# Seven products for the second feed-forward, and a longer run-up to the state-space scan

## The chip, the cores and the metric

The kernel is one launch on one core of a Trainium2 chip. The metric is the device time of a launch in microseconds (us); lower is better. PE is the matrix engine (TensorE), DVE is VectorE, ACT is ScalarE, POOL is GpSimd; SP issues most transfers.

## What is computed

1024 tokens of width 1024 pass through two attention layers and then a second block; the change lies in the second block. All arithmetic is to fp32 accuracy. Cut to what matters:

```
h = h + 0.5 * swiglu(rms_norm(h, ffn1_norm), ...)        # feed-forward 1
u = rms_norm(h, mix_norm)
q, k, v, s_in, gates = split(u @ w_in)                   # the mixer
y_attn = neighbourhood_attention(q, k, v) @ w_attn_out
y_ssm  = s5_branch(s_in) @ w_ssm_out                     # two scans, GELU, GLU
h = h + (sigmoid(g_attn) * y_attn + sigmoid(g_ssm) * y_ssm) @ w_out
h = h + 0.5 * swiglu(rms_norm(h, ffn2_norm), w_gate, w_up, w_down)   # feed-forward 2
h = h + (p @ w_proj) * sigmoid(rms_norm(h, ple_norm) @ ple_w_gate)   # last stage
out = rms_norm(h, final_norm)

swiglu(x) = (silu(x @ w_gate) * (x @ w_up)) @ w_down     # inner width 2816
```

## The kernel before

**Products.** An fp32 operand is kept as a high and a low part (`whi`, `wlo` for weights, `xh`, `xl` for activations), and `mm3` (L188) makes one product of three matmuls: high by high, high by low, low by high (L194 to L196). Accumulators live in PSUM banks named G, S, T and O. `weights` (L162) loads a raw tile (`wraw`) on SP's queue and splits it: POOL writes the high part (L184), POOL or DVE the low part (L186). A PSUM result is split by `split_ps` (L152): ACT writes the high part (L156), DVE the low part (L157).

**Order.** The code is written once in program order; a scheduler that works with its own time estimates orders each engine's instructions and the slots of each pool. `later(n)` marks instructions as filler that may be put off. Each engine runs its list in order, and each instruction waits for semaphores of what it reads or overwrites.

**Mixer** (`mix`, L1304). `ssm_scan` (L1165) loads its input `ssm_u` in eight pieces (L1172), forms the scan's driving terms by PE (L1183, result copied by ACT, L1189), and then runs 127 steps of four small DVE operations each (L1204 to L1208). The result is copied to `se` (L1227 on DVE, L1229 on ACT, 16 each, in four groups q), multiplied on PE (L1235, L1237) and stored. While the scan runs, PE makes q, k and v (`FM`, then the v weights) and the first of 16 gate tiles (`gate`, each 48 matmuls of 512 columns); the gates are put in as filler with `later(20000)`. `ssm_glu` (L1245) then reads the scan's result, and stores `ssm_out`. The neighbourhood attention follows (`attend`, L392): it loads a table `naU`, queries `hq`, keys `hk` and values `hv` on SP; its first product is L449. `ssm_out` (L1383) loads the GLU's result into the slots `xh` that held the mixer's input.

**Feed-forward 2** (`ffn`, L947, called from `second_block`). For each of 22 tiles of 128 inner columns, PE computes gate and up over two halves of 512 tokens (8 feature tiles each, banks G and S); DVE and ACT form the hidden tile and split it (L977 to L987); every second tile, `down` (L960) multiplies by `w_down` into bank T, and DVE adds to the residual h in SBUF (L967). Before it, `mix_out` (L1423) adds the mixer's result to h, and `rms_T` (L934) normalizes (ACT, DVE L945) and transposes on PE (L256) each token tile. After it, `ple` (L1449) is the last stage, with 256-column weights.

## Time and profile before

| | us |
|---|---|
| median of 3 runs (3586.94 to 3595.33) | 3592.09 |
| the profiled execution, its whole time | 3596.7 |
| its span, first to last instruction | 3594.9 |
| PE busy in that span | 3463.1 |

The mixer, from the scan's input to the start of the attention, lies between about 1992 and 2405 us of the span, the attention and the mixer's output until about 2740, the second feed-forward between there and 3470, the last stage behind it. PE's busy time counts pipelined matmuls whole, so a stage with PE busy all the time is read by its number of matmuls and by the distance from start to start.

### The profile page before, as it was taken

To read this page: it belongs to the slowest core of one execution; us is meant where nothing else is said; L and a number is where in the kernel's file an instruction comes from. 1 tells how busy PE (TensorE), PEld (TensorE's weight loads), DVE (VectorE), ACT (ScalarE), POOL (GpSimd) and SP (SyncE) were. 2 spreads that over 40 slices of the span, in tenths; PEclk is the share of its full clock that TensorE was granted. 3 is DMA by queue.
4 is the path that set the end of the run, shared out by engine and by line. 5 is a ranking of instruction groups with operands and counts; after the bars stand their busy time and mean duration, and the time that the engine had idled before them with its cause. 6 is when DMAs were issued, how large, how long until landed. Compare 5 with 4: busy or idle time off the path is not lost. (4 is left out here: it accounts for less than half of the span.)

```text
span 3594.9 us, 53440 instructions
## 1 busy us (share of the span) xinstructions
PE 3463.1 (96%) x19400; PEld 3011.4 (84%) x19400; DVE 2108.4 (59%) x5436; ACT 1072.5 (30%) x2475; POOL 863.1 (24%) x970
## 2 busy tenths in 40 slices
PE   8999999999999999999999898998999999999998
PEld 7988899889889788888888786877798888888888
DVE  5656667646757966666544099428865444444465
ACT  3446645436745310000002310336611000000032
POOL 4233224323213311111112223343222101011112
PEclk9999999999999999999999999999999999999999
DMA  7567763657773222222212732577543111111113
GB/s 228 166 199 218 247 216 109 186 170 234 230 234 114 68 61 62 68 68 60 72 44 86 198 124 91 176 235 199 162 162 91 57 36 59 47 48 53 36 56 115
DMA packets 467671, 456.74 MB, mean 127 GB/s; under 512 B 45760, under 2 KB 354368, under 8 KB 467408
## 3 DMA queue, kind: packets, MB, share of 16 engines
q1 hardware_dynamic: 458192, 442.84, 40.9%
q10 hardware_dynamic: 9216, 10.49, 0.9%
q8 instruction: 154, 2.52, 0.3%
q14 instruction: 109, 0.89, 0.1%
HBM read 335.76 MB, written 117.41 MB: 126 GB/s over the span
## 5 line engine op out<-in xcount | busy, mean ns | idle before, releaser
L184 POOL TENSOR_SCALAR whi<-wraw 128x512 fp32r<-128x512 f32 (+1 forms) x460 | 297.3, 659 | 1903.1 <-PE G L195 837.9
L194 PE MATMUL G<-xh,whi 128*128 128x512 f32 x1472 | 583.9, 397 | 3.5 <-DVE slo L160 2.6
L196 PE MATMUL G<-xh,wlo 128*128 128x512 f32 x1472 | 578.6, 393 | 0.0
L195 PE MATMUL G<-xl,whi 128*128 128x512 f32 x1408 | 553.6, 393 | 0.2 <-DVE xl L157 0.2
L194 PE MATMUL G<-whi,xh 128*128 128x256 f32 (+1 forms) x1536 | 450.2, 293 | 10.2 <-DVE slo L157 5.8
L195 PE MATMUL G<-wlo,xh 128*128 128x256 f32 (+1 forms) x1536 | 444.2, 289 | 0.0
L967 DVE SCALAR_TENSOR_TENSOR h<-T,h 128x512 f32<-128x512 f32 x352 | 242.4, 689 | 333.8 <-PE T L196 331.5
L194 PEld LDWEIGHTS G<-xh,whi 128*128 128x128 f32 x1472 | 278.5, 189 | 62.3 <-DVE slo L160 2.9
L196 PEld LDWEIGHTS G<-xh,wlo 128*128 128x128 f32 x1472 | 277.9, 189 | 56.9
L195 PEld LDWEIGHTS G<-xl,whi 128*128 128x128 f32 x1408 | 266.3, 189 | 51.8 <-DVE xl L157 0.5
L194 PEld LDWEIGHTS G<-whi,xh 128*128 128x128 f32 x1536 | 296.7, 193 | 14.7 <-DVE slo L157 6.2
L195 PEld LDWEIGHTS G<-wlo,xh 128*128 128x128 f32 x1536 | 296.9, 193 | 1.0
L186 DVE TENSOR_TENSOR wlo<-wraw,whi 128x512 fp32r<-128x512 f32 x252 | 200.9, 811 | 118.4 <-POOL whi L184 118.3
L186 POOL TENSOR_TENSOR wlo<-wraw,whi 128x512 fp32r<-128x512 f32 (+1 forms) x208 | 267.8, 1301 | 4.7
L196 PE MATMUL G<-whi,xl 128*128 128x256 f32 (+1 forms) x896 | 262.8, 293 | 0.0
L194 PE MATMUL T<-dhi,hh 128*128 128x512 f32 x640 | 251.2, 393 | 0.0
L196 PE MATMUL T<-dhi,hl 128*128 128x512 f32 x640 | 249.4, 390 | 0.0
L195 PE MATMUL T<-dlo,hh 128*128 128x512 f32 x640 | 249.0, 389 | 0.0
L977 ACT ACTIVATE ft<-G 128x512 f32<-128x512 f32 x88 | 52.6, 597 | 579.9 <-PE G L196 579.8
L986 ACT ACTIVATE hh<-ft 128x512 fp32r<-128x512 f32 x88 | 54.5, 631 | 521.5 <-DVE ft L985 349.7
L194 PE MATMUL S<-xh,whi 128*128 128x512 f32 x512 | 200.2, 391 | 0.0
L196 PE MATMUL S<-xh,wlo 128*128 128x512 f32 x512 | 199.4, 390 | 0.0
(402 smaller groups left out, 7647.7 us busy)
## 6 DMA issues: line engine op xcount, KB each, us to landing
wraw<-w_in SPq DMA_DIRECT2D x144, 256.0 KB, 3.3
draw<-ffn_w_down SPq DMA_DIRECT2D x88, 256.0 KB, 2.6
wraw<-ffn_w_gate SPq DMA_DIRECT2D x86, 256.0 KB, 3.0
wraw<-ffn_w_up SPq DMA_DIRECT2D x86, 256.0 KB, 2.9
wraw<-w_out SPq DMA_DIRECT2D x64, 256.0 KB, 3.3
hk<-ka SPq DMA_DIRECT2D x48, 256.0 KB, 4.9
gs<-gt SPq DMA_DIRECT2D x32, 256.0 KB, 4.0
gl<-gs SPq DMA_DIRECT2D x32, 256.0 KB, 3.9
```

The lines of the kernel that those rows point to most:

```text
L184: self.nc.gpsimd.tensor_scalar(hi, raw, 1.0, 0.0, op0=OP.mult, op1=OP.add)
L186: eng.tensor_tensor(lo, raw, f(hi), op=OP.subtract)
L194: t.matmul(out, lh, rh, start=first and i == 0, stop=False)
L195: t.matmul(out, lh, rl, start=False, stop=False)
L196: t.matmul(out, ll, rh, start=False, stop=last and i == n - 1)
L967: nc.vector.scalar_tensor_tensor(hs, ps, 0.25, hs, op0=OP.mult, op1=OP.add)
L977: nc.scalar.activation(t, pg, AF.Tanh, scale=0.5)
L986: nc.scalar.activation(hh[:, c], t, AF.Copy)
```

## The change

In the second feed-forward the two halves of tokens, of features and of weight columns are taken as 2 x 2 blocks, and x @ w_gate and x @ w_up are made by seven block products instead of eight (`ffn_up`). For this `halves_in` prepares, beside the blocks of x themselves, four sums of them (s1 to s4) for the second half of the tokens, each split into high and low; the weights' block sums t1 to t4 are made on POOL, split by `operand` (ACT high, DVE low) into a ring of half slots, and the products are combined on DVE. Five pairs of products that need only the first half of the tokens are put ahead of the preparation of the second. The hidden values go to DRAM (`hid2`); `ffn_down` then goes over them as four accumulations (two halves of tokens by two halves of columns) of 22 steps, reads and splits the hidden rows once per token half and `w_down` once per accumulation, and POOL writes the low halves of its weights. The residual goes through DRAM (`h2d`, `h3d`) and is loaded again in the last stage. In the mixer, two q tiles stand ahead of the scan's input products, nine gate tiles ahead of its output; the eight loads of `ssm_u` alternate between SP's and ACT's queue; all 32 copies to `se` are on DVE. Weights of 256 and 352 columns begin 32 bytes into their slots (`off=32`, everywhere in the kernel).

```diff
+GATES_FIRST = 9
...
-    def weights(self, src, kt, n, pool=None, tag="w", bufs=4, raws=2):
+    def weights(self, src, kt, n, pool=None, tag="w", bufs=4, raws=2, off=0):
+        o, size = off // 4, 1088 if pool is None else None
...
-            hi, lo = [self.T(pool, [128, 1088 if n == 352 else m * n], F32R, tag + x, bufs)[:, :m * n]
+            hi, lo = [self.T(pool, [128, size or m * n], F32R, tag + x, bufs)[:, o:o + m * n]
                       .rearrange("p (m n) -> p m n", m=m) for x in ("hi", "lo")]
...
-            W = self.weights(win[:, 1632:1888], 8, 256)
+            W = self.weights(win[:, 1632:1888], 8, 256, off=32)
...
+    def halves_in(self, t, src, p, X, tag="T"):
...
+        nc.scalar.activation(a21, ps[0], AF.Copy)
+        self.full(a11, X["a"], slice(0, 4), sl)
+        nc.vector.tensor_tensor(s1, ps[1], a21, op=OP.add)
+        put("b", ps[1])
+        put("s1", s1)
+        nc.gpsimd.tensor_tensor(s1, s1, a11, op=OP.subtract)
+        put("s2", s1)
+        nc.gpsimd.tensor_tensor(a21, a11, a21, op=OP.subtract)
+        put("s3", a21)
+        a12 = tmp("a11")
+        self.full(a12, X["a"], slice(4, 8), sl)
+        nc.vector.tensor_tensor(a12, a12, s1, op=OP.subtract)
+        put("s4", a12)
+    def operand(self, src, lo_eng):
+        if not self.ring:
+            t = [self.T(self.wp, [128, 1024], F32R, x, 4) for x in ("whi", "wlo")]
+            self.ring = [[y[:, c:c + 512] for y in t] for c in (512, 0)]
+        hi, lo = self.ring.pop()
+        as_src = (lambda y: y.rearrange("p (k n) -> p k n", k=4)) if len(src.shape) == 3 else (lambda y: y)
+        self.nc.scalar.activation(as_src(hi), src, AF.Copy)
+        lo_eng.tensor_tensor(as_src(lo), src, as_src(f(hi)), op=OP.subtract)
+        return hi, lo
...
+    def ffn_up(self, X, wg, wu, hid, r, pools, tags):
...
+        def product(W, n):
+            g = tags[turn[0] % len(tags)]
+            turn[0] += 1
+            ps = self.PS(g, bufs[g])
+            self.mm3(ps, self.four(W), x[n])
+            return ps
+        def first(w11, w21):
+            a = tile(r, "r1", 5)
+            nc.scalar.activation(a, product(w11(), "a11"), AF.Copy)
+            c = tile(r, "r2", 5)
+            v.tensor_tensor(c, a, product(w21(), "a12"), op=OP.add)
+            return a, c
...
+        early = {}
+        for j, i in ((0, 0), (0, 1), (1, 0), (1, 1), (2, 0)):
+            early[j, i] = first(corner((wg, wu)[i], j, 0), corner((wg, wu)[i], j, 1))
+            yield
+        p = [pools(0)]
+        spare, stores = None, []
+        def store():
+            for o, k, c in stores:
+                nc.sync.dma_start(hid[o:o + 128, k:k + 512], c)
+            stores.clear()
+        for j in range(11):
+            gates = {}
+            for i, src in enumerate((wg, wu)):
+                top, bot = spare or [self.T(p[i], [128, 4, 256], F32, n, 1) for n in ("top", "bot")]
+                spare = None
+                for k, y in enumerate((top, bot)):
+                    nc.sync.dma_start(y, src[k * 512:k * 512 + 512, j * 256:j * 256 + 256].rearrange("(k p) n -> p k n", p=128))
+                b11, b12, b21, b22 = top[:, :, 0:128], top[:, :, 128:256], bot[:, :, 0:128], bot[:, :, 128:256]
+                t1, t2, t3, t4 = [self.T(p[0], [128, 4, 128], F32, n, 1) for n in ("t1", "t2", "t3", "t4")]
+                if (j, i) in early:
+                    u, c11 = early[j, i]
+                else:
+                    u, c11 = first(lambda: self.operand(b11, v), lambda: self.operand(b21, v))
+                nc.gpsimd.tensor_tensor(t1, b12, b11, op=OP.subtract)
+                nc.gpsimd.tensor_tensor(t2, b22, t1, op=OP.subtract)
+                w, p4 = [], None
+                if len(p) == 1:
+                    nc.gpsimd.tensor_tensor(t4, t2, b21, op=OP.subtract)
+                    nc.gpsimd.tensor_tensor(t3, b22, b12, op=OP.subtract)
+                    w = [self.operand(y, v) for y in (t4, t2, t3, t1)]
+                    yield
+                    p.append(pools(1))
+                    spare = [self.T(p[1], [128, 4, 256], F32, n, 1) for n in ("top", "bot")]
+                    x.update((n, [(hi[:, k], lo[:, k]) for k in range(4)]) for n, (hi, lo) in X.items() if n != "a")
+                    p4 = product(w.pop(0), "b")
+                else:
+                    nc.gpsimd.tensor_tensor(t3, b22, b12, op=OP.subtract)
+                    nc.gpsimd.tensor_tensor(t4, t2, b21, op=OP.subtract)
+                def done(c, hf, n):
+                    if i == 0:
+                        th = tile(p[1], "th", 1)
+                        nc.scalar.activation(th, c, AF.Tanh, scale=0.5)
+                        v.scalar_tensor_tensor(c, th, 1.0, c, op0=OP.add, op1=OP.mult)
+                        gates[hf, n] = c
+                    else:
+                        v.tensor_tensor(c, c, gates[hf, n], op=OP.mult)
+                        stores.append((j * 256 + n * 128, hf * 512, c))
+                done(c11, 0, 0)
+                if i == 0:
+                    store()
+                p6 = product(w.pop(0) if w else self.operand(t2, v), "s2")
+                v.tensor_tensor(u, u, p6, op=OP.add)
+                p7 = product(w.pop(0) if w else self.operand(t3, v), "s3")
+                u3 = tile(p[1], "r3", 2)
+                v.tensor_tensor(u3, u, p7, op=OP.add)
+                p5 = product(w.pop(0) if w else self.operand(t1, v), "s1")
+                c22 = tile(p[1], "r4", 2)
+                v.tensor_tensor(c22, u3, p5, op=OP.add)
+                v.tensor_tensor(u, u, p5, op=OP.add)
+                done(c22, 1, 1)
+                p3 = product(self.operand(b22, v), "s4")
+                v.tensor_tensor(u, u, p3, op=OP.add)
+                done(u, 0, 1)
+                p4 = p4 or product(self.operand(t4, v), "b")
+                v.tensor_tensor(u3, u3, p4, op=OP.subtract)
+                done(u3, 1, 0)
+        store()
...
+    def ffn_down(self, hid, wd, src, dst, p, slots, then, also=None, delay=0):
...
+        for hf in range(2):
+            H = slots(hf) + [(eh[:, k], el[:, k]) for k in range(2)]
+            h = [self.T(p, [128, 1024], F32, "ht", 4) for _ in range(4)]
+            for c in range(2):
+                cs = slice(c * 512, c * 512 + 512)
+                acc = []
+                for t in range(4):
+                    g = "GS"[turn % 2]
+                    turn += 1
+                    acc.append(self.PS(g, self.nG if g == "G" else self.nS))
+                for k in range(22):
+                    hi, lo = H[k]
+                    if c == 0:
+                        for i in range(3) if k == 0 else [k + 2] if k < 20 else []:
+                            raw = self.T(p, [128, 512], F32, "hraw", 3)
+                            (nc.scalar if i < 3 and hf == 0 else nc.sync).dma_start(raw, hid[i * 128:i * 128 + 128, hf * 512:hf * 512 + 512])
+                            nc.scalar.activation(H[i][0], raw, AF.Copy)
+                            nc.vector.tensor_tensor(H[i][1], raw, f(H[i][0]), op=OP.subtract)
+                    raw = self.T(p, [128, 512], F32, "draw", 1) if k % 3 == 2 else self.T(self.wp, [128, 512], F32, "wraw", 2)
+                    nc.sync.dma_start(raw, wd[k * 128:k * 128 + 128, cs])
+                    wh, wl = self.operand(raw, nc.gpsimd)
+                    for t in range(4):
+                        ts = slice(t * 128, t * 128 + 128)
+                        self.mm3(acc[t], [(hi[:, ts], lo[:, ts])], [(wh, wl)], k == 0, k == 21)
+                    if k in (12, 14, 16, 18):
+                        t = (k - 12) // 2
+                        nc.sync.dma_start(h[t][:, cs], src[(hf * 4 + t) * 128:(hf * 4 + t) * 128 + 128, cs])
+                    next(also, None)
+                for t in range(4):
+                    hc = h[t][:, cs]
+                    nc.vector.scalar_tensor_tensor(hc, acc[t], 0.25, hc, op0=OP.mult, op1=OP.add)
+                for t in range(4):
+                    nc.sync.dma_start(dst[(hf * 4 + t) * 128:(hf * 4 + t) * 128 + 128, cs], h[t][:, cs])
...
+            for t in range(4):
+                with self.later(hf * delay):
+                    then(hf * 4 + t, h[t])
...
         for j in range(8):
-            nc.sync.dma_start(u2[j * 16:j * 16 + 16], ud[:, j, :].rearrange("(g i) c -> i g c", i=16))
+            (nc.sync, nc.scalar)[j % 2].dma_start(u2[j * 16:j * 16 + 16], ud[:, j, :].rearrange("(g i) c -> i g c", i=16))
...
+        yield
         yd = self.dr.tile([512, 8, 128], F32, name="ssm_y")
...
                         dst, src = E[e][x * 64:x * 64 + 64, d], X[e * 64:e * 64 + 64, x, d * 16 + q * 4:d * 16 + q * 4 + 4]
-                        if x == e:
-                            v.tensor_copy(dst, src)
-                        else:
-                            nc.scalar.activation(dst, src, AF.Copy)
+                        v.tensor_copy(dst, src)
...
-        yd = self.ssm_scan(sp, ud)
         qd, kd, vd = dr([2, 512, 1024], "naq"), dr([2, 512, 1024], "nak"), dr([1024, 1024], "nav")
-        FM(0, lambda m: self.qk_out(qd, m * 128, -0.125), 4)
-        FM(512, lambda m: self.qk_out(kd, m * 128), 4)
+        FM(0, lambda m: self.qk_out(qd, m * 128, -0.125), (0, 1))
+        scan = self.ssm_scan(sp, ud)
+        with self.tc.issue_after(self.last_mm.ins):
+            next(scan)
+        FM(0, lambda m: self.qk_out(qd, m * 128, -0.125), (2, 3))
+        FM(512, lambda m: self.qk_out(kd, m * 128), range(4))
         for u in range(2):
...
+        FM(2048, gate, range(GATES_FIRST))
+        with self.tc.issue_after(self.last_mm.ins):
+            yd = next(scan)
         with self.later(20000):
-            FM(2048, gate, 16)
+            FM(2048, gate, range(GATES_FIRST, 16))
...
+        h = p.tile([128, 8, 1024], F32, name="h")
+        g = self.rms_gain(p, I["final_norm_2"])
+        for t in range(8):
+            nc.sync.dma_start(h[:, t], hd[t * 128:t * 128 + 128, :])
...
+        h2, hid = dr([1024, 1024], "h2d"), dr([2816, 1024], "hid2")
+        X = {}
         for hf in range(2):
             for u, _ in enumerate(self.mix_out(self.cT, h, hf)):
                 if hf == 0:
-                    load(u + 4, h[:, 0, u * 256:u * 256 + 1])
-            xT.append(self.half(("xh0", "xl0")[hf], ("xh1", "xl1")[hf]))
...
+                    load(u + 4, h[0][:, 0, u * 256:u * 256 + 1])
+            if hf == 0:
+                X["a"] = slot(self.big, "xh0"), slot(self.big, "xh1")
+            else:
+                X.update(b=two(slot(self.big, "xl1")), s1=two(slot(sx, "sc")), s2=two(slot(sx, "sa")),
+                         s3=two(slot(self.big, "xl0")), s4=two(slot(sx, "sb")))
+                up = self.ffn_up(X, I["ffn2_w_gate_2"], I["ffn2_w_up_2"], hid, r, pools(p, 2), "GST")
+                next(up)
+            for t in range(4):
+                if hf == 1:
+                    next(up)
+                x = self.T(p, [128, 1024], F32, "xn", 2)
+                nc.sync.dma_start(h2[(hf * 4 + t) * 128:(hf * 4 + t) * 128 + 128, :], h[hf][:, t])
+                self.rms_tile(h[hf][:, t], x, g)
+                self.halves_in(hf * 4 + t, x, p, X)
+        self.close(hb)
+        next(up)
+        for _ in up:
+            pass
...
+        def then(t, h):
+            if t % 4 == 0:
+                xP.append(self.half(*(("xh0", "xh1"), ("xl0", "xl1"))[t // 4]))
+            self.rms_T(h, rp, g, xP, t)
+        h3 = dr([1024, 1024], "h3d")
+        self.ffn_down(hid, I["ffn2_w_down_2"], h2, h3, p, places(sx, ("xh0", "xh1"), ("xl0", "xl1"), ("sa", "sc", "sb")), then, also(), 400)
+        self.close(p, sx)
+        self.ple(pp, h3, xP, out)
```

**What the order shows.** SP's queue between the scan branch's last stores and the attention's loads. Here `hq`, `hk`, `hv` and `naU` belong to the attention, `xh` receives the GLU's result, `wraw` are weights. Before:

```order
L389 DMA ssm_out<-ghi_25933 128x512
L389 DMA ssm_out<-glt_25930 128x512
L1356 DMA naU_25952<-na_tab 128x1664
L406 DMA hq_25955<-naq 64x512 x2
L420 DMA hk_25958<-nak 64x2x512 x2
L421 DMA hv_25959<-nav 128x4x128
L420 DMA hk_25963<-nak 64x2x256 x2
L421 DMA hv_25964<-nav 128x2x128
L1356 DMA naU_26125<-na_tab 128x1664
L406 DMA hq_26128<-naq 64x512 x2
```

Now:

```order
L392 DMA ssm_out<-ghi_25933 128x512
L392 DMA ssm_out<-glt_25930 128x512
L1610 DMA xh_5018_26091<-ssm_out 128x4x512 x2
L1576 DMA naU_25952<-na_tab 128x1664
L409 DMA hq_25955<-naq 64x512 x2
L423 DMA hk_25958<-nak 64x2x512 x2
L424 DMA hv_25959<-nav 128x4x128
L423 DMA hk_25963<-nak 64x2x256 x2
L424 DMA hv_25964<-nav 128x2x128
L1610 DMA xh_5020_26095<-ssm_out 128x4x512 x2
```

The first two loads of `xh` moved from behind the attention's loads (and behind six loads of weights that follow there) to ahead of them.

PE at the last transposes ahead of the second feed-forward (`T<-ident,xn` is a transpose of a normalized token tile). Before, where the upper tokens' matmuls follow on several banks:

```order
L195 MATMUL S_30149<-xh_5891_29393,whi_30081 128x512
L196 MATMUL S_30149<-xh_5890_29392,wlo_30082 128x512
L256 MATMUL T_30055<-ident,xn_30048 128x128 x4
L256 MATMUL T_30062<-ident,xn_30048 128x128 x4
L194 MATMUL G_30121<-xl_5960_29983,whi_30071 128x512
L194 MATMUL S_30177<-xl_5960_29983,whi_30081 128x512
L194 MATMUL G_30237<-xh_5890_29392,whi_30215 128x512
L195 MATMUL G_30237<-xh_5891_29393,whi_30215 128x512
```

Now, where `xl_5967` holds block b of the upper tokens and `sc` their sum s1:

```order
L198 MATMUL G_30299<-xh_5898_29406,whi_30276 128x512
L199 MATMUL G_30299<-xh_5897_29405,wlo_30277 128x512
L1036 MATMUL T_30321<-ident,xn_30313 128x128 x4
L1036 MATMUL T_30326<-ident,xn_30313 128x128 x4
L197 MATMUL S_30386<-xl_5967_29991,whi_30368 128x512
L197 MATMUL S_30431<-sc_29992,whi_30374 128x512
L198 MATMUL S_30386<-xl_5967_29991,whi_30368 128x512
L199 MATMUL S_30386<-xl_5967_29991,wlo_30369 128x512
```

Before, matmuls of another tile on the lower tokens follow two matmuls behind the transposes; now what follows reads what is made from these transposes, without a matmul on the lower tokens between. Elsewhere PE's rows ahead of the scan's first product count 96 matmuls of the q tiles instead of 70; between the end of v and the first `T<-se` stand 432 gate matmuls instead of 302.

## Rows read from the trace of the kernel before

**Rows 1.** Page, part 1: busy us (share of the span) x instructions.

```profile
PE 3463.1 (96%) x19400; PEld 3011.4 (84%) x19400; DVE 2108.4 (59%) x5436; ACT 1072.5 (30%) x2475; POOL 863.1 (24%) x970
```

**Rows 2.** Windows: stretch, us; busy (x count) per engine; clock, DMA share, GB/s.

```profile
core 0: us, PE busy (x) PEld busy (x) DVE busy (x) ACT busy (x) POOL busy (x), PEclk, DMA share, GB/s
...
3000.00:3050.00 50.00, 50.00 (x222) 41.41 (x221) 23.47 (x35) 3.69 (x6) 6.47 (x10) 1.00 0.18 53
```

**Rows 3.** Timeline of PE: start, us, line, names, [idle before].

```profile
2224.72 0.39 PE L194 MATMUL G<-xh,whi 128*128 128x512 f32 x1
...
2229.02 0.39 PE L195 MATMUL G<-xl,whi 128*128 128x512 f32 x1
2248.02 1.32 PE L1237 MATMUL T<-se,sw 128*128 128x128 f32 x4 [18.61 <-ACT se L1229]
```

**Rows 4.** PE's waits, 1990 to 2420 us: total, times, longest.

```profile
PE T L1237 <- ACT se L1229: 18.6, 1, 18.6
PE S L1183 <- DMA sw<-ssm_win: 8.8, 1, 8.8
```

**Rows 5.** Windows of 10 us in the mixer, columns as in rows 2.

```profile
2010.00:2020.00 10.00, 3.24 (x15) 3.27 (x16) 0.00 (x0) 1.07 (x3) 0.00 (x0) 0.55 1.13 252
...
2230.00:2240.00 10.00, 0.00 (x0) 0.00 (x0) 9.00 (x39) 0.00 (x0) 0.00 (x0) 0.64 0.17 50
...
2410.00:2420.00 10.00, 8.32 (x48) 6.65 (x48) 6.34 (x21) 7.07 (x15) 0.00 (x0) 1.00 1.06 368
```

**Rows 6.** Page, part 5: groups; busy, mean ns of one, idle before.

```profile
L967 DVE SCALAR_TENSOR_TENSOR h<-T,h 128x512 f32<-128x512 f32 x352 | 242.4, 689 | 333.8 <-PE T L196 331.5
...
L186 DVE TENSOR_TENSOR wlo<-wraw,whi 128x512 fp32r<-128x512 f32 x252 | 200.9, 811 | 118.4 <-POOL whi L184 118.3
L186 POOL TENSOR_TENSOR wlo<-wraw,whi 128x512 fp32r<-128x512 f32 (+1 forms) x208 | 267.8, 1301 | 4.7
...
L986 ACT ACTIVATE hh<-ft 128x512 fp32r<-128x512 f32 x88 | 54.5, 631 | 521.5 <-DVE ft L985 349.7
```

**Rows 7.** Timeline of DVE at the scan's end, columns as in rows 3.

```profile
2246.30 0.27 DVE L1204 TENSOR_TENSOR ssm_m<-ssm_x,l 128x64 f32<-128x64 f32 x1
...
2247.34 1.55 DVE L1227 COPY se<-ssm_x 64x516 f32<-64x516 f32 x4
```

**Rows 8.** Groups of DVE, 2070 to 2240 us: busy, mean ns, idle.

```profile
L1204 DVE TENSOR_TENSOR ssm_m<-ssm_x,l 128x64 f32<-128x64 f32 x120 | 39.8, 332 | 13.3 <-ACT ssm_x L1189 9.5
```

**Rows 9.** Timeline of PE at the second feed-forward's start and end.

```profile
2747.22 1.17 PE L256 MATMUL T<-ident,xn 128*128 128x128 f32 x8 [0.80 <-DVE xn L945]
...
3476.91 1.26 PE L256 MATMUL S<-ident,xn 128*128 128x128 f32 x8 [2.03 <-DVE xl L157]
```

**Rows 10.** Groups of DVE, 2730 to 2765 us.

```profile
L157 DVE TENSOR_TENSOR xl<-T,xl 128x512 fp32r<-128x512 f32 x8 | 5.2, 678 | 0.0
L945 DVE SCALAR_TENSOR_TENSOR xn<-h,rrs,rg 128x1024 f32<-128x1024 f32 x3 | 4.1, 1370 | 0.3 <-POOL rrs L539 0.3
```

**Rows 11.** DMA issues, 3000 to 3400 us: count, KB each, us to landing.

```profile
draw<-ffn_w_down SPq DMA_DIRECT2D x26, 256.0 KB, 2.7
```

**Rows 12.** DMA issues, 1995 to 2017 us.

```profile
ssm_u<-ud SPq DMA_DIRECT2D x8, 256.0 KB, 11.5
```

**Rows 13.** Line L1229, ACT's copies: ns least/median/most.

```profile
L1229 ACT ACTIVATE se<-ssm_x x16: 614/624/637, 2247.3 to 2278.3; 64x516 f32<-64x516 f32 x16
```

**Rows 14.** Timeline of SP (queue) at the attention's start.

```profile
2374.52 1.33 SPq L420 DMA_DIRECT2D hk<-nak  x2
...
2401.84 4.39 SPq L1390 DMA_DIRECT2D xh<-ssm_out  x4
```

**Rows 15.** Timeline of PE there: the first product of the attention.

```profile
2405.97 0.73 PE L449 MATMUL S<-hk,hq 128*128 128x512 f32 x2 [0.69 <-ACT tg L1332]
```

**Rows 16.** Page, part 5: two groups of 256 columns.

```profile
L194 PE MATMUL G<-whi,xh 128*128 128x256 f32 (+1 forms) x1536 | 450.2, 293 | 10.2 <-DVE slo L157 5.8
L195 PE MATMUL G<-wlo,xh 128*128 128x256 f32 (+1 forms) x1536 | 444.2, 289 | 0.0
```

More of the change, by code (lines that the diff above doesn't have):

```diff
@@ L195, in mm3 @@
             t.matmul(out, lh, rl, start=False, stop=False)
-            t.matmul(out, ll, rh, start=False, stop=last and i == n - 1)
+            self.last_mm = t.matmul(out, ll, rh, start=False, stop=last and i == n - 1)
     @staticmethod
@@ L661, in keep @@
                 until("cm")
-                W.extend(self.weights(I["w_out"][l, 0:512, u * 256:u * 256 + 256], 4, 256) for u in range(4))
+                W.extend(self.weights(I["w_out"][l, 0:512, u * 256:u * 256 + 256], 4, 256, off=32) for u in range(4))
                 gT.extend(self.T(self.big, [128, 2, 4, 512], F32R, f"xh{h}") for h in range(2))
@@ L760, in out_cm @@
         for u0 in (0, 2):
[L761 removed]
+            W = {u: self.weights(I["w_out"][l, 512:1024, u * 256:u * 256 + 256], 4, 256, off=32) for u in (u0, u0 + 1)}
             for hf in range(2):
@@ L1484, in second_block, with two, slot, pools @@
         nc, I, K = self.nc, self.I, self
+        sb = {}
+        def two(t):
+            return t[:, 0:4], t[:, 4:8]
+        def slot(pool, tag):
+            return K.T(pool, [128, 8, 512], F32R, tag, None if pool is K.big else 1)
+        def pools(old, n):
+            def get(i):
+                if i:
+                    self.close(old)
+                sb[i] = self.pool(f"late{n}{i}", 1, **({} if i else {"side": "right"}))
+                return sb[i]
+            return get
+        def places(sx, even, odd, rest, split=0):
+            def at(hf):
+                a = [slot(self.big, n) for n in (even, odd)[hf]]
+                b = [slot(sx, n) for n in rest]
+                tiles = [two(x) for x in (a[:1] + b + a[1:] if split and hf == 0 else a + b)]
+                return [(hi[:, k], lo[:, k]) for hi, lo in tiles for k in range(4)]
+            return at
         class Next:
@@ L1555, in second_block @@
                 load(k, f(self.cT[1][0][:, k, 0:1]))
-        xT = []
+        self.close(self.gy, self.gp)
+        r = self.pool("r2", 1)
+        p = self.pool("xn2", 1)
+        g = self.rms_gain(p, I["ffn2_norm_2"])
+        for n in ("a21", "a11", "s1"):
+            self.T(p, [128, 4, 128], F32, n, 1)
+        for _ in range(2):
+            self.T(p, [128, 1024], F32, "xn", 2)
+        hb = self.pool("hb", 1, side="right")
+        h.append(hb.tile([128, 4, 1024], F32, name="h1"))
+        h2, hid = dr([1024, 1024], "h2d"), dr([2816, 1024], "hid2")
+        X = {}
         for hf in range(2):
```

113 lines of the change are left out of this document (73 added, 40 removed).

## The prediction

> **What bounds the kernel now.** I read the page's busy shares first: TensorE (PE) is busy 3463.1 of 3594.9 us, no other engine passes 59% [rows 1]. So the time is PE's list of matmuls plus the places where PE stands still; a gain comes from a shorter list or a smaller gap. Next, windows of 50 us over the second feed-forward, of which one of 14 with PE at 50.00 stands in the rows: PE is busy 50.00 of 50.00 at clock 1.00, VectorE (DVE) 23.47 us, ScalarE (ACT) and GpSimd (POOL) under 7, DMA 0.18 [rows 2]. That stage is matmul count alone. One matmul of 512 columns costs there what it takes from start to start: 20 in a row start between 2224.72 and 2229.02 us, 4.30/19 = **0.226 us** each [rows 3]. Third, PE's waits in the mixer: 18.6 us for the scan's output copies, 8.8 us at the scan's first product, put down to the scan's first weights, which are queued right behind the eight loads of its input [rows 4]. The windows around them show PE busy 0.00 of 10 us with a granted clock of 0.64, and 3.24 with 0.55: the clock falls toward its lower level, 1.2 of 2.4 GHz, after PE has stood idle [rows 5].
>
> **Second feed-forward, up half.** Before: 22 tiles x 2 matrices x 2 token halves x 8 k x 3 = 2112 matmuls. After: 11 column pairs x 2 matrices x 7 products x 4 k x 3 = 1848. Removed 264 x 0.226 = **-59.7 us**. What must stay hidden behind the 84 matmuls (19.0 us) of one pair and matrix: on DVE 11 operations with two SBUF inputs (seven low halves, four finishing multiplications) at 0.811 and 7 additions from PSUM at 0.689 = 13.7 us; on POOL four weight sums at 1.301 = 5.2; on ACT seven high halves, a copy and up to four tanh, 12 x 0.631 = 7.6 [rows 6]. All fit, so I cost the additions at nothing in the steady part. The cover is DVE's 5 us of slack.
>
> **A rule against this.** Alone, DVE's first scan operation takes 0.27 us [rows 7]; over the stretch in which POOL prepares weights beside it, it averages 0.332 [rows 8]: sharing lengthens DVE's work by about a fifth there. The Trainium skill, SBUF — State Buffer, section "SBUF: two separate sides", says that a DVE operation with two SBUF inputs and a POOL operation that reads SBUF exclude each other for the whole instruction. By that rule DVE and POOL add up, 13.7 + 5.2 = 18.9 against PE's 19.0: it would just fit. I go by the rows (0.811 is already a mean with POOL at work) and make the rest a rival below.
>
> **Ends of the new stages.** (a) Into the up half: before, the last token tiles cost PE a wait of 0.80 us [rows 9]. After, each tile of the upper tokens needs five splits and three sums in one chain, with single buffers, and five early pairs (120 matmuls, 27.1 us) cover it. In that stretch DVE has about 41 operations at 0.68 to 0.81, two normalizations at 1.37 [rows 6, 10], so 31 to 36 us; and the order puts PE straight from the last transposes to a product that needs the last tile's splits. **+6 us**, between 0 (all hidden) and +14 (a chain of about 9 us per tile, 36 to 41 us against 27). (b) Up to down: hidden rows now come back from DRAM and are split again; their slots overlie closed pools: +3 (0 to +6). (c) Down runs as four accumulations of 22 steps; a step is 12 matmuls, 2.71 us, beside POOL 1.301, ACT 1.26, DVE 0.811 and 256 or 512 KB of loads, each 256 KB 2.7 us to landing in this stage [rows 6, 11], with three raw buffers: hidden. Each change of the four PSUM banks waits for an eviction of 0.689: +4 (0 to +6). (d) Down to the last stage: before, a wait of 2.03 us and smaller ones [rows 9]; after, four tiles' normalizations stand at the end with 60 matmuls of 256 columns ahead of 28 transposes: +2 (-4 to +8). The residual now is reloaded, 4 MB, behind other work: 0. Sum for the feed-forward **-44.7 us**, from -64 to -26.
>
> **Mixer.** (e) 96 matmuls instead of 70 stand ahead of the scan's first product: 26 x 0.226 = 5.9 us of cover in an idle of 9. What PE waits for are the eight loads of the scan's input, 11.5 us each to landing, with the DMA engines filled in that window (share 1.13, 252 GB/s) [rows 5, 12]; they go out on two queues now. The Trainium skill, DMA: Bandwidth & Descriptors, section "Issuing engines are not separate DMA queues", says that this saves issue time alone. The rows agree that the engines, not the issuing, are the limit, so I leave the landing where it is. (f) Ahead of the scan's output stand 432 gate matmuls instead of 302: 130 x 0.226 = 29.4 us of work against 18.6 us of idle [rows 4]. PE then comes at 2229.2 + 29.4 - 5.9 = 2252.7, 4.7 us after the output was ready at 2248.0 [rows 3]: this idle is gone, and the chain behind it starts some 4 us late. Copies: 16 of ACT's at 0.624 become DVE's at 0.39 (1.55 us for four) [rows 7, 13]; the four pieces are chained by loads and products, so 0. (g) What comes back later. The idle removed, 18.6 + 5.9 = 24.5 us, lets PE finish its gates at about 2381 instead of 2405.3. But the attention needs its table, queries and keys. Before, SP sends them right behind the scan branch's last store, keys from 2374.52, and ssm_out's four loads of 1 MB only from 2401.84 [rows 14]. Now two of these stand ahead of the keys on SP, and they wait for that store, some 4 us later, and for the gates' end, since they overwrite the gates' input. Two MB at the 368 GB/s of 2410 to 2420 [rows 5] are 5.7 us. Issue at 2381, 5.7 for the two, 3 more for the keys: first attention product at about 2390 against 2405.97 [rows 15], so **-16 us**, between -25 (the loads hidden after all, both idles kept) and -5 (the 39 us of gates that used to cover the attention's loads are missed further on too).
>
> **Rest.** The 256-column weights start 32 bytes later in their slot. No row shows such a slice; the groups of one shape differ by 4 ns (293 and 289) [rows 16]; half of that over some 5000 matmuls is 10 us. I take 0, with -10 to +10.
>
> **Sum.** -44.7 - 16 = -60.7 us. Against the profiled execution, 3596.7, that is 3536.0; that execution is 4.6 above the median 3592.1 of the three runs, so on the median's scale **3531 us**.
>
> **Rivals.**
> 1. Everything hidden: transitions at nothing, both idles kept: -59.7 - 25 - 4 = -89, 3503 us. For it: ACT and POOL have room throughout. Against it: the order leaves PE no work between the last transposes and the product that needs them.
> 2. Transitions and the attention's start cost their upper ends: -26 - 5 = -31, 3561 us. For it: the loads of the attention are packed at DMA shares near 1 just there, and the tile chain has single buffers.
> 3. Slower than before: in the up half DVE with POOL, not PE, sets the pace. Price: 22 passes x (pass - 19.0 us). It eats the whole 60.7 from 19.0 + 60.7/22 = 21.8 us per pass, that is from 2.9 us of waiting on top of the 18.9 of DVE and POOL in strict turns; at 23.5 us the time is 3531 + 99 = 3630. For it: the lengthened scan steps [rows 7, 8] and the chain of POOL sum, ACT high, DVE low in front of each product. Against it: operands sit in a ring of eight, so the chains overlap, and the rows carry contention already. The Trainium skill's rule on the shared port, cited above, speaks for it.
> 4. The change doesn't do what it says: the nine gate tiles do not stand ahead of the scan's output, and its idle stays: 3531 + 16 = 3547. The order of PE speaks against it.
>
> **How the numbers follow.** Forecast 0.62 (3512 to 3552), rival 1 0.13, rival 2 0.15, rival 3 0.05, rival 4 0.05. The range 3504 to 3566 takes in the forecast, rival 4, nearly all of rival 2 and half of rival 1: about 0.83. A measurement of this kernel tells about 0.2%, 7 us, from no change: faster needs less than 3585. Rivals 1, 2, 4 and the forecast lie there, with 0.01 to 0.02 off their tails: faster 0.93, same 0.03, slower 0.04.
>
> **What would show it.** In the profile after: PE busy near 50 of 50 us through the up half with 220 matmuls each (else rival 3, with DVE near 50); a PE wait of about 6 us before the first product of the upper tokens; no wait at the scan's output, about 3 us at its input; a new wait of about 10 us at the attention's first product, for a DMA. Wrong would be: no wait there (rival 1), or gaps of tens of us inside the up or down half.

## The result, and the profile after

The changed kernel takes **3549.42 us** (median of 4 runs, 3548.84 to 3551.18) against 3593.71 (4 runs) for the kernel before: a ratio of 0.9879, 95% interval 0.9862 to 0.9896, or 44 us less (37 to 50). The forecast was 3531 in a range of 3504 to 3566: right in sign and range, 18 us too hopeful. The profiled execution, 3548.84 us, has a span of 3547.1 us.

Part 1 of the page, as [rows 1]:

```profile
PE 3403.5 (96%) x19136; PEld 2955.0 (83%) x19136; DVE 2181.4 (61%) x5488; ACT 1222.3 (34%) x2739; POOL 1058.2 (30%) x1030
```

PE's list is 264 matmuls shorter, its busy share unchanged. Windows of 50 us, columns as in [rows 2]: the start of the up half (two windows), its steady part, the first two accumulations of the down half, and the end:

```profile
2700.00:2750.00 50.00, 38.66 (x219) 33.22 (x217) 36.99 (x46) 23.57 (x42) 25.55 (x19) 0.91 0.36 116
2750.00:2800.00 50.00, 45.32 (x193) 37.28 (x194) 44.25 (x53) 15.65 (x27) 31.21 (x21) 0.92 0.37 118
2900.00:2950.00 50.00, 50.00 (x222) 41.41 (x221) 32.31 (x47) 14.90 (x26) 14.96 (x10) 1.00 0.29 90
3150.00:3200.00 50.00, 46.36 (x192) 37.58 (x191) 22.19 (x24) 23.50 (x40) 23.18 (x17) 0.93 0.79 256
3200.00:3250.00 50.00, 48.14 (x204) 37.79 (x203) 10.52 (x15) 15.92 (x28) 22.48 (x19) 0.97 0.50 159
3400.00:3450.00 50.00, 43.85 (x317) 41.52 (x316) 27.07 (x47) 14.73 (x37) 9.64 (x15) 0.93 0.51 181
```

In the steady part PE is busy all the time, as in [rows 2], with DVE at 32 us and POOL at 15: the removed matmuls are gained in full. Most of what is missing lies in the other five windows. PE's waits from 1990 to 2420 us, as [rows 4]:

```profile
PE S L452 <- DMA hk<-nak: 12.5, 2, 9.1
...
PE S L197 <- ACT glu_yh L1483: 2.8, 2, 1.7
PE T L1451 <- DVE se L1443: 2.4, 2, 1.5
...
PE S L1399 <- ACT ssm_x L1405: 0.4, 1, 0.4
```

The two long waits of [rows 4] are gone: 2.4 us is left at the scan's output, none over 0.4 at its input. New is the wait for the attention's keys that the prediction named. More than idle time went. From one and the same matmul ahead of the mixer to the point where PE has nothing left but the attention's first product, either kernel has 2177 matmuls. The columns are PE busy (x count), granted clock, DMA share and GB/s, before and after:

```profile
1942.80:2405.30 462.50, 423.57 (x2177) 0.96 0.50 152
```

```profile
1935.60:2363.10 427.50, 415.69 (x2177) 1.00 0.50 155
```

Of 35.0 us, 27.1 are idle time that is gone; in the other 7.9 the same matmuls took less time, at a mean granted clock of 1.00 instead of 0.96 (some 0.9 us of it is the shifted start of 384 matmuls).

PE's waits from 2700 us on:

```profile
PE S L197 <- ACT xl L158: 11.2, 1, 11.2
PE T L1036 <- ACT r L1104: 4.8, 1, 4.8
PE T L259 <- DVE xn L948: 4.2, 2, 2.6
PE G L197 <- ACT xh L1215: 3.5, 1, 3.5
...
PE G L198 <- POOL wlo L1076: 1.8, 4, 0.8
PE G L197 <- DVE ht L1229: 1.6, 1, 1.6
```

The start of the up half, 11.2 + 4.8 = 16.0 us of waiting, is the largest stop left in the program. The 4.8 us are a wait for one of the PSUM banks T, which ACT's copy `r<-T` empties; that copy stands on ACT behind a split that waits 4.32 us for DVE:

```profile
2740.63 0.63 ACT L158 ACTIVATE sb<-a 128x512 fp32r<-128x512 f32 x1 [4.32 <-DVE a L1062]
...
2741.68 0.57 ACT L1104 ACTIVATE r<-T 128x512 f32<-128x512 f32 x1
```

What the traces show by stage, as the excess of PE's time over its matmuls (512 columns at 0.2275 us, 128 at 0.109, 256 at 0.1195 before and 0.1173 after, by mean start-to-start distances), and for the mixer from a matmul of the stage before it to a mark:

| | predicted, us | traces, us |
|---|---|---|
| up half, 264 matmuls fewer | -59.7 | -60 |
| (a) start of the up half | +6 (0 to +14) | +17 (18.7 against 1.7) |
| (b), (c) up to down, four accumulations | +7 (0 to +12) | +14 (6.9, 6.8, 0, 0) |
| (d) end, last stage | +2 (-4 to +8) | +9 (15.0 against 6.3) |
| mixer to the attention's first product | -16 | -26.6 (463.2 against 436.6) |
| mixer to the attention's last product | -16 | -19.2 (669.3 against 650.1) |
| start of the 256-column weights | 0 (-10 to +10) | 2.2 to 2.4 ns in each of some 4800 matmuls |

One profile of the same code can differ from another by some 5 us at a mark like these: the attention's first product, -26.6 here, is at -22 to -24 in the five other kernels below whose mixer is the same up to there, the last product at -15 to -21. So the runs below settle sizes by their medians.

### The profile page after: what moved, and what is told of

It is laid out like the page before. It is cut to its first block, busy times and chain, and to the rows that moved or that the text cites. A ratio compares the mean times of both kernels' runs of the same rounds, so it can differ in the third digit from the quotient of the medians.

```text
span 3547.1 us, 53798 instructions
## 1 busy us (share of the span) xinstructions
PE 3403.5 (96%) x19136; PEld 2955.0 (83%) x19136; DVE 2181.4 (61%) x5488; ACT 1222.3 (34%) x2739; POOL 1058.2 (30%) x1030
## 5 line engine op out<-in xcount | busy, mean ns | idle before, releaser
L197 PE MATMUL G<-whi,xh 128*128 128x256 f32 (+2 forms) x1440 | 425.2, 295 | 13.4 <-ACT xh L1215 3.5
L198 PE MATMUL G<-wlo,xh 128*128 128x256 f32 (+2 forms) x1440 | 418.0, 290 | 1.8 <-POOL wlo L1076 1.8
L199 PE MATMUL G<-whi,xl 128*128 128x256 f32 (+2 forms) x800 | 236.3, 295 | 0.0
L199 PE MATMUL G<-whi,xh 128*128 128x256 f32 (+1 forms) x800 | 230.7, 289 | 0.1
L159 DVE TENSOR_TENSOR ptl<-T,pth 128x512 fp32r<-128x512 f32 (+2 forms) x296 | 181.9, 629 | 20.1 <-ACT pth L158 17.0
L503 PE MATMUL T<-ident,P 128*128 128x128 f32 x1064 | 184.9, 278 | 5.6 <-DVE P L482 4.5
L158 ACT ACTIVATE pth<-T 128x512 fp32r<-128x512 f32 (+2 forms) x296 | 156.1, 553 | 51.7 <-PE T L503 48.1
L510 PE MATMUL O<-pth,hv 128*128 128x256 f32 (+1 forms) x616 | 167.1, 283 | 6.3 <-ACT pth L158 3.1
L452 PE MATMUL S<-hk,hq 128*128 128x256 f32 (+3 forms) x560 | 134.3, 329 | 38.3 <-DMA hk<-nak 12.5
L510 PE MATMUL O<-ptl,hv 128*128 128x256 f32 (+1 forms) x616 | 163.8, 297 | 5.4 <-DVE ptl L159 4.3
```

The source lines that it names most:

```text
L158: nc.scalar.activation(hi, ps, AF.Copy)
L159: nc.vector.tensor_tensor(lo, ps, f(hi), op=OP.subtract)
L197: t.matmul(out, lh, rh, start=first and i == 0, stop=False)
L198: t.matmul(out, lh, rl, start=False, stop=False)
L199: self.last_mm = t.matmul(out, ll, rh, start=False, stop=last and i == n - 1)
L452: nc.tensor.matmul(sc, qt[:, 0, qs], k[:, x, kc], start=x == 0, stop=x == 1)
```

## The experiments

Times are medians, ratios those to runs of the kernel before on the same chip. The runs are spread over several chips and the changed kernel was measured on one of them, so kernels are compared with it by their ratios, 0.9879 (0.9862 to 0.9896) being its own.

**The three parts alone.** The start in the slot:

```diff
-            hi, lo = [self.T(pool, [128, 1088 if n == 352 else m * n], ...)[:, :m * n]
+            hi, lo = [self.T(pool, [128, size or m * n], ...)[:, o:o + m * n]
...
-            W = self.weights(win[:, 1632:1888], 8, 256)
+            W = self.weights(win[:, 1632:1888], 8, 256, off=32)
```

> Only the 32-byte start of the 256- and 352-column weights is taken over from the change; everything else is the kernel before. Up to the mixer both kernels run the same matmuls, and the changed kernel is there 7.3 us ahead; its 256-column matmuls stand 117.7 ns apart against 119.4. Theory A (the start in the slot shortens a 256-column matmul by 1.7 ns or more): about 5000 such matmuls, 7.3 us ahead at the mixer and 9 to 12 us less in all. Theory B (the 7.3 us come from something else in the schedule): within 3 us of the kernel before, slots at 119.4.

3590.59 us, ratio 0.9982 (0.9972 to 0.9992): 6.4 us less (3 to 10). Theory A in kind. Sixteen matmuls in a row of the mixer's output, PE's timeline of the kernel before and of this one (start, us, form):

```profile
2690.81 0.28 PE L195 MATMUL G<-wlo,xl 128*128 128x256 f32 x1
...
2692.61 0.28 PE L195 MATMUL G<-wlo,xl 128*128 128x256 f32 x1
```

```profile
2690.19 0.28 PE L195 MATMUL G<-whi,xl 128*128 128x256 f32 x1
...
2691.95 0.28 PE L195 MATMUL G<-whi,xl 128*128 128x256 f32 x1
```

1.80/15 = 0.120 us before, 1.76/15 = 0.117 with the shifted start. Over 4812 matmuls the mean falls from 119.7 to 117.4 ns, 11 us in all; the medians show about half of that, so part of it is taken up by waits elsewhere. The slots' size, which the edit also sets, is not the cause: the kernel with the feed-forward's part alone (below) has the same slots without the shift, and its 256-column matmuls come at the old distance, 119.5 ns in a count over all matmuls of that width that gives 119.5 before and 117.4 here. How much of the 7.3 us ahead of the mixer is the shift's is not shown: that kernel without a shift comes to the program's ten-thousandth matmul at 1716.0 us, against 1722.1 before and 1714.9 in the changed kernel, and kernels with one and the same code up to there spread over 5 us.

The mixer's part, on the kernel before (its hunks of `ssm_scan` and `mix`):

> Only the mixer's part of the change (two q tiles ahead of the scan's input, nine gate tiles ahead of its output, copies on VectorE, input loads on two queues), no 32-byte start, feed-forward before. Theory A (the parts are independent, and the changed kernel's attention gives back 7 us of the 26 that its start is ahead): 17 to 21 us less. Theory B (the prediction's term, first attention product only 16 us earlier and nothing given back later): 16 less, with the attention's length unchanged at 206 us from its first product to its last.

3580.36 us, 0.9951 (0.9938 to 0.9965): 17 us less. The attention's first product comes 20.6 us earlier against the mixer's start, its last 14.7. The 20.6 us are 25.5 of idle time removed and 4.9 by faster matmuls (mean granted clock 0.99 instead of 0.96), less some 10 us of waiting for the keys. The attention then takes 5.9 us longer, as theory A has it, with 5.5 us in three more waits for keys where the kernel before has 0.5:

```profile
PE S L450 <- DMA hk<-nak: 16.0, 4, 10.5
```

The feed-forward's part, with the mixer and the weight starts of before:

> Only the second feed-forward's part of the change, mixer and weight starts as before. By the two traces the removed matmuls give 60 us back and the stage's start (a wait of 16.5 us), its middle (12 us more than its matmuls in the down half) and its end take about 33: theory A, the parts are independent: 22 to 28 us less than before. Theory B (the wait at the start is made by the shifted mixer): the wait is under 8 us here and the gain over 35.

3576.29 us, 0.9939 (0.9924 to 0.9953): 21 us less, just under theory A's range. PE's waits at the start of the up half are the changed kernel's to a tenth:

```profile
PE S L196 <- ACT xl L157: 11.2, 1, 11.2
PE T L1035 <- ACT r L1103: 4.8, 1, 4.8
```

So that wait belongs to this part alone. 6.4 + 16.6 + 20.7 = 43.7 us: the parts add up to the whole.

**Loads on two queues.**

```diff
-            (nc.sync, nc.scalar)[j % 2].dma_start(u2[j * 16:j * 16 + 16], ...)
+            nc.sync.dma_start(u2[j * 16:j * 16 + 16], ...)
```

> The changed kernel with all eight loads of the scan's input on SP's queue again. Theory A (the DMA engines, not the issuing, limit these loads; the two q tiles ahead are what removes the wait): first product of the scan at most 2 us later, time within 3 us of the changed kernel. Theory B (two queues bring the input earlier): the last load lands 4 us or more later and the time is 4 us or more above the changed kernel.

3546.08 us, 0.9871 (0.9852 to 0.9890): no difference in time. Against the mixer's start the scan's first product comes 3.1 us later than in the changed kernel, 0.9 to 3.1 later than in all profiles with this mixer and two queues, with this wait in PE's list:

```profile
PE S L1399 <- DMA sw<-ssm_win: 2.8, 1, 2.8
```

With two queues this wait is at most 0.8 us in any profile, so second queue and q tiles remove it together. No gain in time is seen, but 3 us are less than these intervals can tell. The Trainium skill, DMA: Bandwidth & Descriptors, section "Issuing engines are not separate DMA queues", would have it that only issue time is saved; the runs agree as far as time goes.

**Half of the copies on ScalarE again.**

```diff
-                        v.tensor_copy(dst, src)
+                        if x == e:
+                            v.tensor_copy(dst, src)
+                        else:
+                            nc.scalar.activation(dst, src, AF.Copy)
```

> The changed kernel with half of the copies of the scan's result on ScalarE again, as before. By the prediction's term the copies are worth nothing: first product of the scan's output and first product of the attention within 1 us of the changed kernel, time within 3 us (theory A). Theory B (16 copies in a row on VectorE hold back the output's first products, as waits of 1.7 and 1.1 us there suggest): with two engines the first product comes 1 to 2 us earlier, and the attention's first product too. Theory C (ScalarE's slower copies, 0.62 against 0.42 us, and its place in the chain of the four pieces count): 3 us or more later at the attention's first product.

3573.04 us, 0.9939 (0.9924 to 0.9954): 22 us slower than the changed kernel. The attention's first product comes 17 us later, which is theory C by its sign, but not by the mechanism that it names. ACT's timeline (start, us, [idle before]) and PE's wait around the scan's end:

```profile
2239.16 2.33 ACT L1446 ACTIVATE se<-ssm_x 64x516 f32<-64x516 f32 x4 [28.85 <-DVE ssm_x L1424]
2241.39 0.57 ACT L1552 ACTIVATE tg<-G 128x512 f32<-128x512 f32 x1
```

```profile
PE G L197 <- ACT tg L1552: 16.0, 1, 16.0
```

The copies stand on ACT ahead of the gate tiles' evacuations and wait 28.85 us for the scan's last step (L1424); the evacuations (`tg<-G`) wait behind them with both G banks of PSUM full, and PE stops in the middle of the gate tiles that were to fill this time. The four copies cost 2 us; their place on an in-order queue costs 16. By the time this kernel loses all that the mixer's part had won: the attention's last product stands 671.8 us behind the mixer's start, against 669.3 before and 650.1 in the changed kernel.

**Attention's loads first.**

```diff
+              with self.tc.issue_after(self.vl[1].ins):   # behind the first head's values
                 nc.sync.dma_start(f(t)[:, i], sd[i, :, ...])
```

> The changed kernel with the loads of ssm_out queued on SP behind the first attention head's queries, keys and values, as before, instead of ahead of them. Theory A (2 MB ahead of the keys delay the attention's first product; PE's wait there is 9.3 us in the changed kernel): the first product comes 4 to 6 us earlier, the wait is 3 to 5 us, and the time falls by 2 to 6 us. Theory B (the loads are needed anyway and the same delay shows up at the products that read ssm_out or at the next head): the first product comes earlier, but the last product of the attention and the time stay within 2 us.

3548.96 us, 0.9864 (0.9845 to 0.9883). In the changed kernel SP sends ssm_out's loads ahead of the keys:

```profile
2357.70 1.00 SPq L1610 DMA_DIRECT2D xh<-ssm_out  x2
...
2360.78 1.27 SPq L423 DMA_DIRECT2D hk<-nak  x2
```

Turned round, PE's waits between 2340 and 2420 us are:

```profile
PE S L452 <- DMA hk<-nak: 5.2, 2, 3.6
...
PE G L198 <- DMA xh<-ssm_out: 1.3, 1, 1.3
```

The first product comes 5 to 10 us earlier than in the changed kernel and the five others with this mixer, the wait falls from 9.1 to 3.6 us. Some is lost again at once, at the products that read ssm_out. The time is 5 us lower by the ratios, within their intervals: likely, not shown.

**The start of the up half.** Four kernels on the 16.0 us. First weights behind the third tile:

```diff
-        next(up)
+        with self.tc.issue_after(m[0]), self.tc.issue_after(m[1]), self.tc.issue_after(m[2]):
+            next(up)      # m: last split (ACT, DVE) and sum (POOL) of tile 6; of tile 7 in the second kernel
```

> The changed kernel with the first weights of the upper tokens (four sums on GpSimd, five splits on ScalarE and VectorE) queued behind the splits of the third of the four upper token tiles instead of in the middle of them. Theory A (PE's wait of 16.5 us at the start of the up half comes from these weights standing ahead of tiles three and four on the in-order engines): the wait falls by 4 to 7 us and the time by as much, to about 0.9865 of the kernel before. Theory B (the chain of one tile with its single buffers sets the wait): the wait stays within 2 us of 16.5.

3554.37 us, 0.9876 (0.9855 to 0.9896), PE's waits:

```profile
PE S L197 <- ACT whi L1077: 13.5, 1, 13.5
PE T L1036 <- DVE xl L159: 2.7, 1, 2.7
```

Behind the last tile:

> The same weights queued behind the splits of the last tile on all three engines. Theory A: the last tile's splits are ready 8 us or more earlier, but the four weight sums (5.2 us) and the first splits then follow them, so the wait falls by 2 to 4 us only. Theory B: the tiles are not ready earlier, and the wait grows by 5 us or more, to over 21.

3557.20 us, 0.9892 (0.9872 to 0.9913):

```profile
PE T L197 <- ACT whi L1077: 18.6, 1, 18.6
PE T L1036 <- DVE xl L159: 2.7, 1, 2.7
```

16.2 and 21.3 us. Theory A falls: the weights' place among the tiles is not the cause; they are needed as soon as the tiles. Three early pairs instead of five:

```diff
-        for j, i in ((0, 0), (0, 1), (1, 0), (1, 1), (2, 0)):
+        for j, i in ((0, 0), (0, 1), (1, 0)):
```

> The changed kernel with three early pairs of products instead of five: 48 matmuls, 10.9 us, move from ahead of the wait to behind it. Theory A (a chain of fixed length on DVE, ACT and POOL, covered by the early products): the wait grows from 16.5 to 24 to 27 us and the time by 7 to 11. Theory B (the early products' own splits, additions and copies sit in the chain and lengthen it about as much as they cover): the wait grows by less than 4 us.

3561.14 us, 0.9900 (0.9883 to 0.9916), some 8 us more than the changed kernel:

```profile
PE G L197 <- ACT xl L158: 17.0, 1, 17.0
PE T L1036 <- DVE xl L159: 4.8, 1, 4.8
PE T L1036 <- ACT a L1051: 2.8, 2, 2.5
```

10.9 us of cover less, and some 9 us more waiting. The first product of the upper tokens comes 46.2 us after the mixer's last matmul, against 46.4 in the changed kernel: a chain of fixed length, which early products cover nearly one to one. The 8 us in the time lie within the two intervals. Transposes first:

```diff
-                if hf == 1:
-                    next(up)
                 x = self.T(p, [128, 1024], F32, "xn", 2)
...
                 self.halves_in(hf * 4 + t, x, p, X)
+                if hf == 1:
+                    with self.tc.issue_after(self.last_tr.ins):
+                        next(up)
```

> The changed kernel with each upper tile's transposes ahead of the next early pair of products on PE, instead of behind it: PE's list is the same, the first of these transposes comes about 9 us earlier, and 24 early matmuls (5.5 us) stand behind the last transposes. Theory A (the chain of ACT, DVE and POOL work that makes the upper tokens' blocks has a fixed length and starts late, because PE's order holds the first transposes back while its token tile has long been normalized): PE's wait at the start of the up half falls from 16.5 us to 6 to 10, the time by 6 to 10 us. Theory B (DVE and POOL are full in this stretch, so an earlier start changes nothing at the end): the wait falls by less than 3 us.

3545.19 us, 0.9869 (0.9840 to 0.9898):

```profile
PE T L197 <- DVE xl L159: 7.2, 1, 7.2
PE T L1036 <- DVE r L1106: 1.9, 1, 1.9
PE S L197 <- ACT xl L158: 0.7, 1, 0.7
```

9.8 us of waits instead of 16.0, but the first product of the upper tokens comes only 2.2 us earlier after the mixer's last matmul (44.2 against 46.4 us), with part of the same matmuls now run in between; the time is 4 us lower by the ratios, within their intervals. The late transposes are a part, then. What makes the rest is not shown. From the mixer's last matmul to that product the windows are, columns as in [rows 2], in the changed kernel and here:

```profile
2708.20:2754.70 46.50, 30.48 (x150) 25.04 (x148) 36.65 (x44) 21.91 (x40) 25.29 (x18) 0.85 0.33 103
```

```profile
2715.80:2760.00 44.20, 34.41 (x150) 27.35 (x148) 32.33 (x43) 21.12 (x39) 23.67 (x18) 0.85 0.37 119
```

DVE has 10 to 12 us idle in it, so theory B's full engines are not the whole answer either. The wait that is left (7.2 us) is again one for bank T, which transposes and early products share and which a split on DVE must empty; no run gave them separate banks. DVE's work there is lengthened by POOL. Its groups in the changed kernel from 2705 to 2760 us (busy, mean ns):

```profile
L1076 DVE TENSOR_TENSOR wlo<-t,whi 128x512 fp32r<-128x512 f32 x4 | 5.8, 1482 | 0.0
...
L159 DVE TENSOR_TENSOR xl<-T,xl 128x512 fp32r<-128x512 f32 x4 | 2.7, 685 | 0.4 <-ACT xl L158 0.3
```

One and the same split, first while POOL stands idle (from 2750.81 to 2754.67), then beside one of its sums:

```profile
2751.28 0.68 DVE L159 TENSOR_TENSOR sa<-s,sa 128x512 fp32r<-128x512 f32 x1
...
2754.67 1.28 POOL L1066 TENSOR_TENSOR a<-xh,xh 128x512 f32<-128x512 f32 x1 [3.85 <-DVE sb L159]
...
2758.95 1.61 POOL L1066 TENSOR_TENSOR a<-xh,xh 128x512 f32<-128x512 f32 x1
...
2759.58 1.54 DVE L159 TENSOR_TENSOR sa<-s,sa 128x512 fp32r<-128x512 f32 x1 [0.15 <-ACT sa L158]
```

All of this shape (128x512) in the stretch agree: with two inputs in SBUF they take 0.68 to 0.69 us where POOL does no sum (11 operations) and 0.94 to 1.76 where it does one throughout (5), the other 13 lying between 0.68 and 1.78; with an input from PSUM 0.67 to 0.69 either way (13). This is what the Trainium skill, SBUF — State Buffer, section "SBUF: two separate sides", leads one to expect of such pairs, and the trace agrees. Up to the first product it makes DVE's work some 8.6 us longer. No run took POOL's sums away, so how much of the wait this makes is not shown.

**The down half's first steps.**

```diff
-        store()
+        store(nc.gpsimd)
```

> The changed kernel with only the last four stores of hidden rows issued from GpSimd's queue instead of SP's. In the changed kernel the third weight load of the down half is issued on SP right behind these stores, which wait for the last product, and ScalarE then waits for that load in front of the hidden rows' splits; PE waits 3.7 us there and runs some 3 us at a lower clock. Theory A (that queue order makes the wait): the wait falls under 1 us, the time by 3 to 6 us. Theory B (the loads' traffic or the slots make it): the wait stays over 3 us.

3552.94 us, 0.9884 (0.9869 to 0.9898): nothing gained. PE's longest waits there (3.5 us in the changed kernel), and SP's queue:

```profile
PE G L197 <- ACT xh L1215: 4.5, 2, 3.4
```

```profile
3140.11 4.53 SPq L1218 DMA_DIRECT2D wraw<-ffn_w_down  x2
3154.86 0.33 SPq L1218 DMA_DIRECT2D draw<-ffn_w_down  x1
```

SP is free from 3144.6, and still sends the load of the third weights at 3154.86: these stores are no longer ahead of it. By the code it waits for its slot (`draw`), which overlies what the up half used to its end, and the time fits: VectorE's last operation of the up half ends at 3154.80. In the changed kernel ACT shows what that does, waiting 5.08 us in order for that load while two more hidden rows, landed at 3141.92 and 3149.83, stand behind it:

```profile
3152.87 0.63 ACT L1075 ACTIVATE whi<-draw 128x512 fp32r<-128x512 f32 x1 [5.08 <-DMA draw<-ffn_w_down]
```

**Both turned orders together** (`attn_first` and `tr_first`):

> The changed kernel with two orders undone or turned: the loads of ssm_out queued behind the first head's queries, keys and values, and the upper tiles' transposes ahead of the next early pair on PE. Theory A (the two places are independent): the 5.5 us and 3.9 us of PE's waits that each removed alone add up, to about 9 us less than the changed kernel, a ratio to the kernel before of 0.985 to 0.986. Theory B (a gain at the attention's start is given back behind it): no better than the changed kernel with the transposes alone, 0.987.

3548.04 us, 0.9855 (0.9838 to 0.9873): the best ratio, 9 us under the changed kernel's by the two ratios, but their intervals overlap. Both waits are shorter in its profile, where the changed kernel has 12.5 us for the keys and 11.2 in its longest at the up half:

```profile
PE S L452 <- DMA hk<-nak: 7.1, 3, 4.5
```

```profile
PE T L197 <- DVE xl L159: 7.2, 1, 7.2
```

Against it stands that the attention's last product comes later there than in the other kernels with this mixer (659.5 us behind the mixer's start, against 646 to 655); this profile is of the longest of the kernel's four runs (3556.18). The sum of two gains is likely, not shown.

## Why the prediction was right, and where it missed

- **The up half's removed matmuls, -59.7: right.** PE stays at 50.00 of 50 us with 222 matmuls, and rival 3 (DVE with POOL setting the pace) is out: DVE is at 32 us of 50, with the contention in it.
- **Step (a), the start of the up half, was mis-sized and beyond its bound:** +6, at most +14, and it is +17. The mechanism, single-buffered chain against 27 us of cover, was right. The 6 us are about what DVE's list (31 to 36 us) exceeds the cover by, as if DVE began with the cover and never stood still. Its list is 36.7 us, at or just over the top of that, with 8.6 us in it from POOL's sums beside it, where I had priced 0.68 to 0.81 us per operation throughout. Idle time of DVE inside the chain, 9.9 us, I had put at nothing; so too the lower clock of the first products after the wait, some 3 us (18.7 us of excess against 16.0 of waiting). PE's order, which holds the first transposes behind 42 early matmuls, is worth 2.2 us at the first product.
- **Steps (b) and (c), +7 against +14:** the mechanism of (b), slots under closed pools, fits what the runs show; the price lacked the in-order wait on ACT behind the one late load, and the lower clock after it (0.93 and 0.97 in the two windows). In (c) the loads are not hidden at the start of the second accumulation: PE waits 1.8 us there for POOL's low halves, which follow ACT's high halves, which wait up to 4.1 us for a load of weights, and the clock is 0.83 from 3220 to 3230 us. The change to the third accumulation costs 1.6 us, the last one nothing.
- **Step (d), +2 against +9:** four tiles' normalizations at the end wait 4.2 us, others follow in the last stage, at a clock of 0.93 to 0.97; its upper end was +8. No run tested this.
- **The mixer, -16, was right by luck:** 17 us alone, from two misses that cancel. Step (f) (the idle at the scan's output gone) and step (g) (the keys come late behind ssm_out's loads) stood in the profile as described, the wait being 9.1 us where I had named about 10. Step (e) was too cautious: the wait at the input is gone altogether. But the first product was to come 16 us earlier, at most 25, and comes 20.6 to 26.6 earlier: I counted idle time alone and put the faster matmuls, 5 to 8 us once the clock no longer falls there, at nothing. And what the attention gives back, 5.9 us by later waits for keys, stood only in my upper bound. "Copies: 0" holds for their duration and fails for their place: without that edit the mixer's part gains nothing.
- **The 32-byte start, 0 with -10 to +10:** 6.4 us less, inside the bound.
- Together the feed-forward gave 21 us instead of 44.7, outside the -64 to -26 that I had allowed; the slots and the cancelling misses of the mixer kept the total inside the range, nearer to rival 2 (3561) than to the forecast. In that the total's fit is luck too.

## What to carry to other kernels

A copy that waits long costs what stands behind it on its engine's queue, not what it takes: put it on the engine that is waiting for the same thing anyway. Where a stage of fewer matmuls needs more preparation, price its first pass by itself, from durations with the neighbouring engine at work, and count from where PE's order releases it; the steady state says nothing on the two ends. Cover for such a chain paid nearly one to one here, while the chain was longer than its cover. And an idle of the matrix engine costs more than its length where the granted clock falls with it, here 5 to 8 us on top of some 26: count the slower matmuls too.

## What the hardware showed that was not expected

A matmul of 256 columns comes every 119.7 ns with its weights at the start of their slot and every 117.4 ns with the start moved by 32 bytes (means over 4820 and 4812 matmuls), while those of 352 columns stay at 160.3 with or without it. The eleven kernels with the shift agree with each other within 0.2 ns, and so do the three without it. Why is open.
